# A hybrid decoder block on one core: first weights in quarters, taps read from E, operand fills in phases, and the branches' joins in the last pair's place

## The chip, the cores and the metric

The kernel runs on one core of one Trainium2 chip. The metric is the device time of one execution in microseconds (us): the median over several executions. Lower is better. One execution has also been recorded by the hardware profiler; its views are what this document quotes. The engines are PE (matrix multiplications), PEld (its weight loads, beside PE), DVE (elementwise work on two tensors), ACT (copies, scalings, activations), POOL (here it only issues DMAs and makes a few masks) and SP (here it only issues DMAs).

## The reference, cut to what matters

All tensors are float32, with 256 tokens of 4096 channels.

```python
h = rmsnorm(x, norm_w)
u_p, z_p, u_c, b_c, c_c, z_c, g_logit = split(h @ w_in)      # 20480 columns
y_pool = causal_multiscale_pool(u_p, pool_w, pool_scale) * silu(z_p)   # 2048
y_conv = b_c * conv3(c_c * u_c) * silu(z_c)                  # 2048, causal, width 3
br = [y_pool @ w_branch[0], y_conv @ w_branch[1]]            # 2 x 4096
gates = sigmoid(g_logit + gate_b)                            # 2 x 4096
merged = gates[0] * br[0] + gates[1] * br[1]
out = rmsnorm(x + merged @ w_out, final_norm_w)
```

## The kernel before

**Units and steps.** The work is cut into units of 1024 output columns, in this fixed order: cz0, cb0, cu0, cc0, the same four for cz1 (the convolution mixer's projections), pz0, pu0, pz1, pu1 (the pooling mixer's), g0_0, g1_0, ... g1_3 (eight units of gate logits), b0_0, b1_0, ... b1_3 (the two branch products, in turn for each quarter c of the columns), and o0 to o3 (the output product). A unit of w_in or w_out has 16 steps, a branch unit has 8. A step takes one weight tile of 256 rows by 1024 columns (1 MB, seen as four cells of 128x512) and multiplies it with the matching 256 channels of the 256 tokens.

**Float32 out of rounded halves.** Every float32 operand is split into a high part (rounded to the type that PE takes) and a low part (the rest). A product is three matmuls: high by high, high by low, low by high. ACT writes the high parts (`highs`, L185, through `act` at L54), DVE subtracts to get the low ones (`lows`, L189, through `tt` at L57). The parts lie in a ring of 15 cells. The weight tile itself lands in one of three raw slots of 1 MB.

**P and S steps.** A P step is 8 products, 24 matmuls. An S step is Strassen's form in the variant of Winograd: 7 products, 21 matmuls, but DVE must first make four sums of the weight cells (`parts`), of which ACT and DVE then make high and low parts too. A P operand takes 4 KB a partition in the arena, an S operand 7 or 8. The order of P and S within a unit is a string (`SIX4`, `EIGHT`, `B0`, `B1`, ...). The four E banks of PSUM (`sums`) take one output block each, the four F banks (`shared`) the products that serve several blocks. After the last S step ACT copies the F banks ("corners") into a raw slot, which the unit's `Join` object takes in the order of the loads; DVE makes three corner sums there, and adds them to the evacuated E banks (`combine`, L357).

**What sets the order.** All engines execute in the order in which the Python program issues instructions (`pin`). That order is made by hand: after each group of matmuls `after_group` (L919) evacuates banks that are complete, counts matmuls, and calls `tick` once for every 6. A tick pops one item of the queue of epilogue work and calls `pop_fill` (L702). Then `pump` (L875) issues what it may: the next weight load, when the raw slot's last user has been prepared, and the preparation (highs, sums, lows) of steps up to `limit`, which is four steps ahead, and only two at the last step of a unit that has `urgent` work (L932). `urgent` work is issued in `combine`, right behind the joins.

**The opening.** The first unit runs 16 P steps whose first operands are the scaled columns of x. For eight of them x is staged: ACT scales into `sa` (`x_scale`, L805), DVE makes four sums, a cast and a difference (`x_sums` and `fill_staged`, L811 and L655). `x_scale` of step j lies in the `pre` list of step j-1, ahead of its highs, and `x_sums` in its `mid` list, behind its lows (L825 to L830). The first weight tile is loaded in two halves (L866).

**Convolution taps.** At the end of cc0 and cc1 (`c_epi`, L462) PE transposes E into the F banks, two items apart; for each bank ACT writes the scaled middle tap to Y and four DVE instructions (`stt`, L69) add the other two taps, reading the bank in PSUM.

**Operand fills.** The operands of the branch and output products (8 + 8 + 16) go through DRAM and come back during the last gate unit and later. `Fill` objects fetch one into a stage (`sa`, later `sb` too) and, six or more ticks later, fill it whole: for an S operand four sums, a cast and a difference, all on DVE; for a P operand a cast on ACT and a difference on DVE. Only the head of the list is looked at. The last four operands of the output product are `Direct`: `fill_direct` (L664) makes them from Y in one go on DVE, without DRAM.

**Branches.** After b0_c DVE multiplies the branch with its gate into Y, and POOL stores that in DRAM (`p_d`, 1 MB). After b1_c DVE multiplies E with its gate, and POOL gathers `p_d` into E with an adding DMA. Then come transposes and the store to `m_d` (L596 to L619).

## Time and profile before

| what | value |
|---|---|
| median of 3 runs | 2462.22 us (2459.26 to 2463.23) |
| the profiled execution | 2464.99 us |
| its span, first to last instruction | 2463.3 us |
| mean granted clock of PE | 0.989 |
| matmul instructions of PE | 10515 |

The profile is of one execution. Its page has the busy time of each engine, a strip of 40 slices, and a chain of work followed back from the last instruction. The trace behind it answers by groups of instructions (busy time, mean length, the idle time before them and who ended it), by timeline (start, length, engine, line of the kernel, operation, output from input, count, and in brackets the idle time before the row and its releaser) and by windows (busy time and, in brackets, instructions of each engine in a stretch, then the granted clock of PE, the share of the DMA engines, and GB/s). Matmuls have L913, transposes L394, ACT's work L54, DVE's L57, L69 and L653.

### The profile page before, as it was taken

Reading aid. Unit: us, or ns where it says so; the run is one execution under the profiler, and the core shown is the slowest. Engines: PE = TensorE matmul, PEld = TensorE weight load, DVE = VectorE, ACT = ScalarE, POOL = GpSimd, SP = SyncE. Lnnn points to the kernel's source line nnn. Section 1 sums busy time; section 2 is a strip of 40 time slices with the busy share of each in tenths; the row PEclk is TensorE's granted clock in tenths of the full one; section 3 lists DMA queues with packets and bytes.
Section 4 is the critical chain, followed back from the end, with each engine's and each line's share of the span. In section 5 each row is a group of like instructions: output and inputs, shape, how many; then the busy total and the mean of one; then the engine's idle time right before and its main releaser. Section 6 shows DMA issues by size and latency. Waiting matters only on the chain.

```text
span 2463.3 us, 26875 instructions
## 1 busy us (share of the span) xinstructions
PE 2389.8 (97%) x10515; PEld 1966.2 (80%) x10515; DVE 2131.9 (87%) x1780; ACT 1410.6 (57%) x1358; POOL 91.8 (4%) x154
## 2 busy tenths in 40 slices
PE   7999999999999999999999999999999998999998
PEld 6888887888878888888888888887777776778886
DVE  6888889888988969969998899979868778899998
ACT  4656555656555656555666566655645545456664
POOL 0000000000000000000000000000000001000000
PEclk9999999999999999999999999999999999999999
DMA  7656457555645655655676567767667677658767
GB/s 280 250 205 222 179 183 254 201 193 208 225 182 204 232 189 193 224 196 189 247 256 229 197 241 258 239 205 260 233 239 282 205 251 244 215 179 267 243 220 269
DMA packets 83791, 553.36 MB, mean 225 GB/s; under 512 B 9552, under 2 KB 9552, under 8 KB 22096
## 3 DMA queue, kind: packets, MB, share of 16 engines
q1 hardware_dynamic: 68832, 484.47, 54.0%
q0 software_dynamic: 14400, 66.07, 9.5%
q8 instruction: 82, 1.34, 0.2%
q10 hardware_dynamic: 432, 1.11, 0.1%
q14 instruction: 45, 0.37, 0.0%
HBM read 522.25 MB, written 29.36 MB: 224 GB/s over the span
## 4 chain that ended last, share of the span: by engine, by line
PE 77%; DVE 12%; DMA 4%; ACT 4%; issue 3%; DVEq 0%; SPq 0%; ACTq 0%; POOL 0%; POOLq 0%
PE sums L913 57%; PE shared L913 18%; DVE ring L57 5%; DMA raw<-in_w_branch_dram 2%; ACT ring L54 2%; DVE parts L57 1%; DVE raw L57 1%; DVE E L57 1%; PE shared L570 1%; ACT raw L54 1%; ACT E L54 1%; DVE arena L57 1%; DMA raw<-in_w_in_dram 1%; DVE sa L57 0%; DVE Y L69 0%
## 5 line engine op out<-in xcount | busy, mean ns | idle before, releaser
L913 PE MATMUL sums<-ring,arena 128*128 128x512 f32 x7881 | 1850.7, 392 | 39.9 <-DVE ring L57 25.2
L913 PEld LDWEIGHTS sums<-ring,arena 128*128 128x128 f32 x7881 | 1486.7, 189 | 358.8 <-DVE ring L57 32.1
L57 DVE TENSOR_TENSOR ring<-raw,ring 128x2048 fp32r<-128x2048 f32 (+3 forms) x526 | 937.8, 1796 | 195.0 <-ACT ring L54 194.5
L54 ACT ACTIVATE ring<-raw 128x2048 fp32r<-128x2048 f32 (+3 forms) x526 | 790.8, 1520 | 521.9 <-PE sums L913 231.4
L54 ACT ACTIVATE ring<-parts 128x1024 fp32r<-128x1024 f32 (+1 forms) x402 | 399.7, 1009 | 360.2 <-DVE parts L57 323.0
L913 PE MATMUL shared<-ring,arena 128*128 128x512 f32 x2268 | 551.5, 392 | 18.5 <-DVE ring L57 9.8
L913 PEld LDWEIGHTS shared<-ring,arena 128*128 128x128 f32 x2268 | 426.5, 189 | 111.9 <-DVE ring L57 13.2
L57 DVE TENSOR_TENSOR ring<-parts,ring 128x2048 fp32r<-128x2048 f32 (+3 forms) x224 | 434.6, 1953 | 40.6 <-ACT ring L54 39.9
L57 DVE TENSOR_TENSOR parts<-parts,raw 128x512 f32<-128x512 f32 x378 | 262.0, 693 | 12.9
L57 DVE TENSOR_TENSOR parts<-raw 128x1024 f32<-128x1024 f32 x189 | 230.5, 1220 | 26.7 <-DMA raw<-in_w_branch_dram 21.3
L57 DVE TENSOR_TENSOR raw<-raw 128x512 f32<-128x512 f32 (+1 forms) x90 | 78.1, 868 | 14.7 <-ACT raw L54 12.7
L54 ACT ACTIVATE raw<-shared 128x512 f32<-128x512 f32 x120 | 64.2, 614 | 11.2 <-DVE ring L57 10.8
L54 ACT ACTIVATE E<-sums,rin 128x512 f32<-128x512 f32 x56 | 36.1, 689 | 25.4 <-PE sums L913 25.4
L69 DVE SCALAR_TENSOR_TENSOR E<-raw,rin,E 128x1024 f32<-128x1024 f32 x28 | 34.7, 1282 | 0.5
L54 ACT ACTIVATE E<-sums 128x512 f32<-128x512 f32 x44 | 24.6, 596 | 12.1 <-PE sums L913 11.2
L78 POOL DMA_DIRECT2D E<-in_rows_dram x16 | 13.8, 864 | 441.7 <-DVE E L69 439.5
L54 ACT ACTIVATE sa<-Y,par 128x256 f32<-128x256 f32 x16 | 7.3, 502 | 35.7 <-DVE extra L57 16.0
L57 DVE TENSOR_TENSOR arena<-sa,arena 128x512 fp32r<-128x512 f32 (+2 forms) x28 | 24.9, 890 | 2.5 <-ACT arena L54 1.8
L57 DVE TENSOR_TENSOR E<-E,raw 128x2048 f32<-128x2048 f32 x11 | 25.2, 2292 | 0.4
L57 DVE TENSOR_TENSOR E<-E,Y 128x2048 f32<-128x2048 f32 x11 | 25.2, 2290 | 0.3
L570 PE MATMUL shared<-ring 128*128 128x512 f32 x96 | 22.1, 389 | 0.0
L570 PEld LDWEIGHTS shared<-ring 128*128 128x128 f32 x96 | 18.0, 188 | 3.7
(114 smaller groups left out, 442.7 us busy)
## 6 DMA issues: line engine op xcount, KB each, us to landing
raw<-in_w_in_dram SPq DMA_DIRECT2D x319, 1024.0 KB, 4.8
raw<-in_w_branch_dram SPq DMA_DIRECT2D x64, 1024.0 KB, 6.2
raw<-in_w_out_dram SPq DMA_DIRECT2D x64, 1024.0 KB, 5.1
E<-in_rows_dram POOLq DMA_DIRECT2D x16, 512.0 KB, 10.0
gates_d<-E POOLq DMA_DIRECT2D x8, 1024.0 KB, 7.1
Y<-gates_d POOLq DMA_DIRECT2D x8, 1024.0 KB, 7.1
Y<-in_xc_dram SPq DMA_DIRECT2D x16, 256.0 KB, 5.2
E<-in_x_dram POOLq DMA_DIRECT2D x4, 1024.0 KB, 5.6
```

Source lines behind the costliest of these rows:

```text
L54: return pin(nc.scalar.activation(dst, src, func, **kw))
L57: return pin(nc.vector.tensor_tensor(out=dst, in0=a, in1=b, op=op))
L69: return pin(nc.vector.scalar_tensor_tensor(out=dst, in0=a, scalar=s, in1=b, op0=op0, op1=op1, **kw))
L78: return pin(nc.gpsimd.dma_start(dst, src, accum_op=ALU.add))
L570: pin(nc.tensor.matmul(o, a, b, start=(k, i) == (0, 0), stop=(k, i) == (3, 2)))
L913: pin(nc.tensor.matmul(ps, lhs, rhs, start=n == 0, stop=n == u.total[b] - 1))
```

## The change

1. The first weight tile is loaded in four quarters; its highs, lows and matmuls go cell by cell. `x_scale` moves from `pre` to `mid`, behind the lows of the step before. The squares of x's rows come two steps later, and the root goes to `mid` of the last step.
2. The taps: ACT first copies the four F banks to E, when the transposes of all of them are done; the taps read E.
3. Fills go in phases, one for each tick: an S operand has sums (DVE), a copy (ACT), a difference (DVE); a P operand the last two. `pop_fill` takes the first fill that may advance, not only the head. The direct fills are gone: all 16 operands of the output product go through `m_d`.
4. The arena loses its last region of 8 KB; a tile of its own, `last_pair`, stands for it. From b0_0 to b1_3 it holds the corners of b0_c (so that its join takes no raw slot), and then the gated b0_c, which DVE adds to E after b1_c. `p_d`, its stores and its adding gathers are gone. `urgent` no longer multiplies; the multiplications stand at the head of the epilogue. The lookahead at the last step of a branch unit is 3 and not 2.
5. `corner_sums` runs as soon as all corners are copied, not only in `combine`. A join that takes a raw slot stands one to two loads earlier among the loads where the unit before ends in P steps.
6. B1 is PSPSPSPP and not PSPPSPPS; the operands of branch two lie accordingly, three P operands in the places of two S operands (`("q", i)`).

The diff, cut to its core:

```diff
-B1 = "PSPPSPPS"
+B1 = "PSPSPSPP"
@@ Step.first, Step.rest (the same for lows)
                 if self is steps[0]:
-                    for i in (slice(0, 2), slice(2, 4)):
-                        highs(cells[i], self.q[:, i])
+                    for i in range(4):
+                        highs(cells[i:i + 1], self.q[:, i:i + 1])
@@ Step.groups
             if self is steps[0]:
                 for k in (1, 0):
-                    cells = self.cells[2 - 2 * k:4 - 2 * k]
-                    for i in range(3):
-                        for n in (1, 0):
+                    for n in (1, 0):
+                        cell = self.cells[2 * (1 - k) + 1 - n]
+                        h, l = high(cell), low(cell)
+                        for i in range(3):
                             for t in range(2):
@@
+    def corner_sums(u):
+        copy_corners(u)
+        if u.cornered or u.pending or u.join.slot is None or not u.closed(FB):
+            return
+        u.cornered = True
+        q = u.join.slot
+        add(q[:, 0], q[:, 2], q[:, 0])
+        add(q[:, 3], q[:, 0], q[:, 3])
+        sub(q[:, 0:2], q[:, 1:2].to_broadcast([P, 2, NH]), q[:, 0::3])
@@ conv_units, c_epi
-            items = gap(6)
+            def copy(j):
+                if j == 3:
+                    for i in range(4):
+                        act(chan(E)[:, 2 * i:2 * i + 2], bankview(i))
             def taps(j):
-                v, y = bankview(j), chan(Y)
+                v, y = chan(E)[:, 2 * j:2 * j + 2], chan(Y)
...
-            for f in transposes(E, taps):
-                items += [f, None]
+            items = gap(6) + pairs(transposes(E, copy)) + gap(2)
+            for j in range(4):
+                items += [lambda j=j: taps(j), None]
@@ branch_unit
             if n == 0:
-                return []
+                return gap(1) + [lambda: mul(parked_sum(), E, Y)]
...
-        def urgent():
-            if n == 0:
-                mul(Y, E, Y)
-                move(p_d[c], Y)
-            else:
-                mul(E, E, Y)
-                for t in range(2):
-                    gather(E[:, t], p_d[c][:, t])
+            def stored():
+                put(m_d[c], chan(Y))
+                merged[c] = now[0] + STORED
+            return [lambda: mul(E, E, Y), None, add_parked] + gap(11) + pairs(transposes(E, copy)) + [stored]
+        def add_parked():
+            add(E, E, parked_sum())
...
-        u.urgent = urgent
+        u.urgent, u.lead = (lambda: None), 3
+        if n == 0:
+            u.rotates = False
@@ class Fill (class Direct, fill_direct and fill_staged are gone)
+        def advance(self):
+            o, q = self.o, self.st[:, 0:self.o.n] if self.o.kind == "S" else self.st[:, 4:8]
+            if self.phase == 0 and o.kind == "S":
+                sums_s(self.st)
+                self.phase = 1
+            elif self.phase < 2:
+                act(o.view[:, 0], q)
+                self.phase = 2
+            else:
+                sub(o.view[:, 1], q, o.view[:, 0].bitcast(F32))
+                self.phase = 3
+                o.ready = True
+                fills.remove(self)
@@ pop_fill
+        for f in list(fills):
+            if f.at is not None and f.free() and (now[0] >= f.at + LANDING or f.o is force):
+                f.advance()
+                break
@@ opening
         if j in staged:
-            steps[j - 1].pre.append(item(x_scale, j))
-            steps[j - 1].mid.append(item(x_sums, j))
+            steps[j - 1].mid += [item(x_scale, j), item(x_sums, j)]
...
-        before(4 + 3 * c, square, c)
+        before(6 + 3 * c, square, c)
...
-    before(14, root)
+    steps[15].mid.append(item(root))
@@ loaded
-        loaded += mine[:3] + ([units[v - 1].join] if v and units[v - 1].s else []) + mine[3:]
+        before_it = units[v - 1] if v else None
+        at = 3
+        if before_it and before_it.main:
+            while before_it.main[len(before_it.main) - 1 - (3 - at)].kind == "P" and at > 1:
+                at -= 1
+        loaded += mine[:at] + ([before_it.join] if v and before_it.s and before_it.rotates else []) + mine[at:]
@@ issue_load
         if i == 0:
-            for k in range(2):
-                load(r[:, k * NU:(k + 1) * NU], s.src[:, k * NU:(k + 1) * NU])
+            for k in range(4):
+                load(r[:, k * NH:(k + 1) * NH], s.src[:, k * NH:(k + 1) * NH])
@@ after_group
-        copy_corners(u)
+        if u.s and u is not last:
+            corner_sums(u)
...
         if u.urgent and st is u.steps[-1]:
-            state["limit"] = state["now"] + 2
+            state["limit"] = state["now"] + u.lead
```

## The prediction

> **What bounds the kernel now.** I read the page's busy times first, then the chain of work, then the groups of instructions (for who ends PE's idle time), then windows over the whole span.

> ```profile
> PE 2389.8 (97%) x10515; PEld 1966.2 (80%) x10515; DVE 2131.9 (87%) x1780; ACT 1410.6 (57%) x1358; POOL 91.8 (4%) x154
> ```
> ```profile
> 118.05 7.48 PE sums L913 x33
> ```
> ```profile
> L913 PE MATMUL sums<-ring,arena 128*128 128x512 f32 x7881 | 1850.7, 392 | 39.9 <-DVE ring L57 25.2 <-ACT ring L54 9.8 <-ACT E L54 4.5
> ```
> ```profile
> L913 PE MATMUL shared<-ring,arena 128*128 128x512 f32 x2268 | 551.5, 392 | 18.5 <-DVE ring L57 9.8 <-DVE Y L69 8.7
> ```
> ```profile
> 40.00:360.00 320.00, 319.18 (x1413) 263.06 (x1412) 276.59 (x253) 188.87 (x184) 12.16 (x31) 1.00 0.60 220
> 360.00:400.00 40.00, 35.83 (x154) 28.47 (x153) 36.94 (x38) 17.73 (x20) 0.65 (x2) 0.91 0.53 196
> 400.00:700.00 300.00, 299.52 (x1329) 247.49 (x1328) 262.89 (x201) 177.88 (x164) 1.95 (x3) 1.00 0.58 208
> 700.00:740.00 40.00, 35.06 (x154) 28.09 (x153) 36.89 (x38) 17.77 (x21) 0.54 (x1) 0.96 0.54 197
> 740.00:1660.00 920.00, 919.82 (x4103) 761.88 (x4102) 809.85 (x633) 552.90 (x513) 30.14 (x41) 1.00 0.63 220
> 1660.00:1745.00 85.00, 77.17 (x328) 61.92 (x327) 76.45 (x74) 51.60 (x49) 8.70 (x15) 0.98 0.69 242
> 1745.00:2170.00 425.00, 394.73 (x1706) 321.72 (x1705) 341.24 (x294) 214.57 (x217) 26.23 (x41) 0.97 0.68 236
> ```

> PE is busy 97%. Its pace where nothing is missing is 7.48 / 33 = 0.2267 us a matmul (chain row). The number of matmuls does not change, so all that can be won is idle time, 39.9 + 18.5 = 58.4 us in the two groups, and the slower clock behind it. The windows say where that lies. I charge each instruction 0.2267 us and take the rest of the window as lost. From 40 to 360, 400 to 700 and 740 to 1660 nothing is lost. 360 to 400 and 700 to 740 lose 40 - 154 x 0.2267 = 5.1 each (end of cc0 and cc1, the taps). 1660 to 1745 (g1_3, start of b0_0) loses 85 - 74.4 = 10.6. 1745 to 2170 (all branches, start of o0) loses 425 - 386.7 = 38.3, of it 30.3 idle. The opening comes on top. Every edit is costed against these places.

> **The opening.** The weight loads' lengths are medians of the first 20 us; the timelines are of ACT, DVE and PE.

> ```profile
> 2.18 8.76 DMA Y<-in_xc_dram
> ```
> ```profile
> raw<-in_w_in_dram SPq DMA_DIRECT2D x3, 1024.0 KB, 10.6
> ```
> ```profile
> raw<-in_w_in_dram SPq DMA_DIRECT2D x2, 512.0 KB, 5.9
> ```
> ```profile
> 10.96 0.91 ACT L54 ACTIVATE sa<-Y,par 128x256 f32<-128x256 f32 x2 [6.15 <-DMA Y<-in_xc_dram]
> 11.77 1.99 ACT L54 ACTIVATE ring<-raw 128x1024 fp32r<-128x1024 f32 x2
> 18.48 0.91 ACT L54 ACTIVATE sa<-Y,par 128x256 f32<-128x256 f32 x2 [4.72 <-DVE extra L57]
> 19.30 3.70 ACT L54 ACTIVATE ring<-raw 128x2048 fp32r<-128x2048 f32 x2
> ```
> ```profile
> 15.12 1.02 DVE L57 TENSOR_TENSOR sa<-sa 128x128 f32<-128x128 f32 x4
> 16.18 0.63 DVE L653 CAST arena<-sa 128x896 fp32r<-128x896 f32 x1
> 16.84 1.09 DVE L57 TENSOR_TENSOR arena<-sa,arena 128x896 fp32r<-128x896 f32 x1
> ```
> ```profile
> 23.57 5.03 PE L913 MATMUL sums<-ring,arena 128*128 128x512 f32 x14 [1.82 <-DVE ring L57]
> ```

> Step 0's weights, issued ahead of the x columns of 2.18, are there by 2.2 + 5.9 = 8.1; their highs wait until 11.77 behind `x_scale`, which waited for those columns. The second `x_scale` (18.48) waits for DVE to empty `sa`, and step 1's highs (19.30) wait behind it. The new order puts step 0's highs ahead of `x_scale`, and step 1's ahead of the second one. Step 1 then has two inputs. Its x: 10.94, some 0.9 later for two more issues ahead of it, + 0.91 scale + 3.3 on DVE (the three rows and the extra column) = 16.1. Its weights: issued near 3.5, + 10.6 = 14.1, + 1.85 highs (half of 3.70) + 2.29 lows = 18.3. So step 1 is in full run at 18.3 and not at 23.57: 5.3, and with the 1.82 gap the clock dip behind it goes: **+6.5**, between +4 (quarters land no earlier than halves, x is later) and +8.5. The row fetch "later" changes nothing: POOL's first fetch has nothing to wait for in either order. SP's later loads wait for the same slots.

> **The taps.**

> ```profile
> 384.54 2.24 PE L913 MATMUL shared<-ring,arena 128*128 128x512 f32 x6 [1.99 <-DVE Y L69]
> 388.56 1.62 PE L913 MATMUL shared<-ring,arena 128*128 128x512 f32 x3 [1.78 <-DVE Y L69]
> ```
> ```profile
> 380.00:400.00 20.00, 16.23 (x61) 12.46 (x60) 19.72 (x23) 8.21 (x9) 0.09 (x1) 0.83 0.56 198
> ```
> ```profile
> L69 DVE SCALAR_TENSOR_TENSOR Y<-shared,par,Y 128x255 f32<-128x255 f32 (+1 forms) x32 | 14.5, 478 | 0.6
> ```
> ```profile
> E<-g_d POOLq DMA_DIRECT2D x2, 1024.0 KB, 7.6
> ```

> PE waits because the taps still read banks that it wants: 8.7 us in all four stalls (the "DVE Y L69" of the second group). The copies free the banks, so these stalls go. But the 16 taps of a unit are still 7.6 us of DVE, and DVE has only 0.28 us free in these 20: what is late next is the lows behind the taps. E is also in use longer: POOL's load of `g_d` into E waited for the transposes and now waits for the last tap on DVE. It takes 7.6, and the multiplication that needs it stands 6 ticks behind, 36 matmuls or 8.2 us, and lows behind that on DVE; up to 2 us of new wait there. I take half of what the two places lose: **+5.5**, between +1 (the whole wait moves to the ring) and +12 (20 - 61 x 0.2267 = 6.2 lost in this window, twice). [...]

> **Fills in phases, g1_3 and the start of b0_0.**

> ```profile
> 1733.75 6.55 PE L913 MATMUL sums<-ring,arena 128*128 128x512 f32 x21 [4.52 <-ACT E L54]
> ```
> ```profile
> 1730.67 0.65 ACT L54 ACTIVATE arena<-sa 128x512 fp32r<-128x512 f32 x1
> 1731.19 1.93 ACT L54 ACTIVATE ring<-raw 128x2048 fp32r<-128x2048 f32 x1
> 1732.99 2.44 ACT L54 ACTIVATE E<-sums,rin 128x512 f32<-128x512 f32 x4
> ```

> An S fill loses its 0.63 cast on DVE and gets a copy on ACT instead, 0.65 x 896/512 = 1.1. What matters is the order: DVE sums, ACT copy, DVE difference, with ACT in program order. Here PE waits 4.52 because the E banks are evacuated behind a P fill's copy and one highs of 1.93. In the new order an S fill's copy stands in that place, and its sums stand on DVE behind two lows (4.5) and the corner sums (2.67, below): queued behind this one ACT instruction are highs of step 2 and the evacuation that PE waits for. I expect 8 to 10 where 4.52 stands, and small stalls in g1_3 (85 - 77.17 - 4.52 = 3.3 now) to change places: **-6.5**, between -10 and +1 (the copy finds its sums done).

> **Branch boundaries.**

> ```profile
> 1780.43 2.67 DVE L57 TENSOR_TENSOR raw<-raw 128x512 f32<-128x512 f32 x3
> 1783.14 2.29 DVE L57 TENSOR_TENSOR E<-E,raw 128x2048 f32<-128x2048 f32 x1
> 1785.47 2.29 DVE L57 TENSOR_TENSOR Y<-E,Y 128x2048 f32<-128x2048 f32 x1
> 1787.68 4.49 DVE L57 TENSOR_TENSOR ring<-raw,ring 128x2048 fp32r<-128x2048 f32 x2
> ```
> ```profile
> 1790.02 11.17 PE L913 MATMUL sums<-ring,arena 128*128 128x512 f32 x48 [1.89 <-DVE ring L57]
> ```
> ```profile
> 2069.89 14.67 PE L913 MATMUL sums<-ring,arena 128*128 128x512 f32 x53 [6.99 <-DVE ring L57]
> ```
> ```profile
> 2159.25 3.78 PE L913 MATMUL shared<-ring,arena 128*128 128x512 f32 x8 [6.02 <-DVE ring L57]
> ```

> PE waits 1.89 for step 2's lows, which stand behind 2.67 + 2.29 + 2.29 of join and gate. With the lead of 3 they stand ahead of the last two, 4.58: this stall goes. Next late is step 3, whose load comes after the join has given its slot back; where b0 ends its join has none now, and the load comes without delay; where b1 ends it still does. `p_d` gone takes 8 MB of transfers from these bursts and costs DVE four adds of 2.29, covered by its 425 - 341.24 = 84 idle in the stretch, except in its last unit. Of the 38.3 lost from 1745 on, 6.99 and 6.02 are idle in b1_3 and o0; of the other 17.3 idle and 8 of slow clock some 14 lie at the boundaries up to b0_3: **+11**, between +4 and +15.

> **b1_3 and o0.** b1_3's 6.99 stands behind fills on DVE and a late load; the fills are as many as before, plus the add. o0's start also gets the pattern of b0_0: **-2.5** (-6 to +5). In o0 6.02 comes from four direct fills ahead of the lows; they go through DRAM now, and are done ticks later and before the steps that use them. With the clock behind it and the neighbouring stalls: **+9.5** (5 to 11).

> **At nothing:** corner sums ahead of lows at the boundaries of the other units, and earlier joins there; PE has 0.18 idle in the 920 us from 740 on, and DVE 110 to cover 2.67 each time; without that cover each boundary would cost up to 2.67. B1's order has the same 5 P and 3 S.

> **Sum:** 6.5 + 5.5 - 6.5 + 11 - 2.5 + 9.5 = 23.5. The profiled execution took 2464.99 us (span 2463.3), 2.8 over the median; 2464.99 - 23.5 = 2441.5, and against the median 2462.22 - 23.5 = **2438.7**.

> **The rivals.**
> - *The starts don't stall.* If DVE has run ahead, the S fills' copies find their sums done, and the two starts cost nothing extra; the rest then comes near its upper ends: 6.5 + 8 + 13 + 10.5 + 0 = 38, **2424**. For it: ACT is 57% busy. Against: DVE has 8.6 free of 85 in that stage.
> - *It does not do what it says.* DVE stays the bound: taps +1, boundaries +4, fills -6.5, o0 +5, and only the opening 6.5 is real: 10, **2452**. For it: 25.2 of the 39.9 already end at DVE's ring.
> - *Slower: the phases stop DVE.* Each of 13 S fills (5 for branches, 8 for the output product) makes DVE wait for ACT's copy behind one highs: 1.1 + 1.93 - 0.63 = 2.4, where DVE has no reserve; with the slow clock as in the taps' window (6.2 lost on 3.77 idle, 1.6 times) 3.8 of PE. All other gains make 32.5 without the two start terms; from 9 of 13 fills on it is slower. All 13: 50 lost, 17 net, **2479**. Against: DVE has 84 free in the branches.

> **How the numbers follow.** Forecast 0.45 (2431 to 2447 by itself), starts don't stall 0.22, DVE stays the bound 0.18, phases 0.15. The range 2418 to 2460 leaves out the last rival and the far ends. About 0.2%, 4.9 us, is what a measurement of this kernel tells from no change. Faster: the first two and two thirds of the third, 0.79; same: the rest of it and a few fills, 0.08; slower: 0.13.

> **What would show it.** Right: step 1 in full run near 18; no wait on "DVE Y" at L69; b0_0's first matmul later behind "ACT E" by 4 to 5 than now; 1.89 at b1_0's step 2 gone; no stall of 6 in o0. Wrong: a gap at the taps' place with releaser "DVE ring" as large as before, DVE idle behind "ACT arena" in many rows, or new idle time from 740 to 1660.

## The result, and the profile after

| | before | after |
|---|---|---|
| median of 4 runs | 2461.56 us (2459.26 to 2463.23) | 2442.16 us (2441.45 to 2444.01) |
| profiled execution, span | 2464.99, 2463.3 | 2441.96, 2440.2 |

The ratio of after to before is 0.9923, 95% interval 0.9906 to 0.994: 19.4 us faster by the medians. The two profiled executions differ by 23.0, since that of before is 3.4 above its median and that of after is not.

The page's busy times of after, and the two groups of PE that carried the idle time (the page's costliest groups):

```profile
PE 2382.4 (98%) x10515; PEld 1959.1 (80%) x10515; DVE 2130.3 (87%) x1756; ACT 1430.8 (59%) x1380; POOL 86.3 (4%) x148
...
L935 PE MATMUL sums<-ring,arena 128*128 128x512 f32 x7515 | 1760.0, 391 | 38.2 <-ACT E L54 17.9
...
L935 PE MATMUL shared<-ring,arena 128*128 128x512 f32 x2100 | 509.5, 391 | 5.0 <-DVE ring L57 5.0
```

From the view of waits (us in all, times, the longest):

```profile
PE sums L935 <- ACT E L54: 17.9, 3, 8.7
PE sums L935 <- DVE ring L57: 15.8, 12, 3.6
```

PE's idle time in the two groups fell from 58.4 to 43.2, and its make-up changed: "DVE Y" is gone, "DVE ring" fell from 25.2 + 9.8 to 15.8 + 5.0, and "ACT E", the evacuation of the E banks, went from 4.5 to 17.9. To see where the time came from, I took from both traces the moment at which PE begins the same step, and subtracted. Steps are counted from 0, and the last column is the prediction's term.

| PE begins | before | after | gained so far | in this part | forecast |
|---|---|---|---|---|---|
| cb0 (the opening is over) | 108.36 | 102.00 | 6.4 | +6.4 | +6.5 |
| cz1 | 356.10 | 349.91 | 6.2 | -0.2 | 0 |
| cz1, step 7 (taps of cc0 are over) | 401.93 | 392.05 | 9.9 | +3.7 | +2.75 |
| pz0 | 696.55 | 686.92 | 9.6 | -0.3 | 0 |
| pz0, step 7 (taps of cc1 are over) | 742.37 | 729.15 | 13.2 | +3.6 | +2.75 |
| g1_3 | 1641.39 | 1629.35 | 12.0 | -1.2 | 0 |
| b1_0 (g1_3 and b0_0 are over) | 1777.54 | 1772.94 | 4.6 | -7.4 | -6.5 |
| b1_3 | 2052.32 | 2036.62 | 15.7 | +11.1 | +11 |
| o0 | 2107.24 | 2093.51 | 13.7 | -2.0 | -2.5 |
| o1 | 2206.05 | 2182.51 | 23.5 | +9.8 | +9.5 |
| end of the span | 2463.28 | 2440.23 | 23.05 | -0.5 | 0 |

The places that were put at nothing lose 2 in all, and no stall over 0.3 stands there. The matmuls that read an operand in `last_pair` are slower in the changed kernel:

```profile
L935 PE MATMUL sums<-ring,last_pair 128*128 128x512 f32 x366 | 89.8, 396 | 0.0
```

From 740 to 1660 one begins every 0.234 us, the others every 0.227, as all did before. Over the 534 of them (366 and 168) that is 3.8 us, an estimate from these two figures: a price of part 4 that the prediction did not have.

The opening, in the timelines of ACT and of PE after:

```profile
14.24 1.91 ACT L54 ACTIVATE ring<-raw 128x2048 fp32r<-128x2048 f32 x1 [1.60 <-DMA raw<-in_w_in_dram]
```
```profile
18.53 4.82 PE L935 MATMUL sums<-ring,arena 128*128 128x512 f32 x14 [1.82 <-DVE ring L57]
```

Step 1 is in full run at 18.53, 23.57 before. Its highs now wait for the weights alone, which land just ahead of 14.24. The taps, in PE's timeline and in windows:

```profile
385.39 1.43 PE L935 MATMUL sums<-ring,arena 128*128 128x512 f32 x5 [0.86 <-DVE ring L57]
386.66 1.07 PE L935 MATMUL shared<-ring,arena 128*128 128x512 f32 x4
389.42 2.11 PE L935 MATMUL shared<-ring,arena 128*128 128x512 f32 x8 [1.69 <-DVE ring L57]
```
```profile
380.00:400.00 20.00, 17.44 (x76) 13.78 (x76) 19.76 (x20) 10.79 (x10) 0.56 (x1) 1.00 0.63 240
```

The stalls of 1.99 and 1.78 behind "DVE Y" became 0.86 and 1.69 behind "DVE ring", two steps later. DVE is as full as before (19.76 of 20), and the granted clock is 1.00 where it was 0.83. At the starts of b0_0 and o0 the stall grew; this is PE and then ACT and DVE at b0_0:

```profile
1726.79 13.58 PE L935 MATMUL sums<-ring,arena 128*128 128x512 f32 x49 [8.67 <-ACT E L54]
```
```profile
1717.38 1.08 ACT L54 ACTIVATE raw<-shared 128x512 f32<-128x512 f32 x2
1723.41 0.95 ACT L54 ACTIVATE arena<-sa 128x896 fp32r<-128x896 f32 x1 [4.96 <-issue]
1724.27 1.89 ACT L54 ACTIVATE ring<-raw 128x2048 fp32r<-128x2048 f32 x1
1726.07 1.25 ACT L54 ACTIVATE E<-sums,rin 128x512 f32<-128x512 f32 x2
```
```profile
1717.52 2.29 DVE L57 TENSOR_TENSOR ring<-raw,ring 128x2048 fp32r<-128x2048 f32 x1 [0.48 <-ACT ring L54]
1719.73 2.67 DVE L57 TENSOR_TENSOR raw<-raw 128x512 f32<-128x512 f32 x3
1722.32 1.01 DVE L57 TENSOR_TENSOR sa<-sa 128x128 f32<-128x128 f32 x4
1726.19 2.29 DVE L57 TENSOR_TENSOR ring<-raw,ring 128x2048 fp32r<-128x2048 f32 x1 [2.86 <-ACT ring L54]
```

The fill's copy (arena from sa) starts the moment DVE has its sums done (1722.32 + 1.01), and DVE came to them behind a lows and the corner sums. "Issue" is the page's word for a wait that it has no releaser for; DVE's row shows what it was. Behind the copy stand a highs and then E. DVE in turn idles 2.86 for that highs. At o0 a copy (0.95, behind DVE) and a highs (1.89) stand ahead of E in the same way; ahead of both, ACT waits 7.99 for a load of `w_out`, and DVE for the highs of that load:

```profile
2093.51 11.79 PE L935 MATMUL sums<-ring,arena 128*128 128x512 f32 x44 [7.91 <-ACT E L54]
```

### The profile page after: what moved, and what is told of

The parts are those of the page before. It is cut to its first block, busy times and chain, and to the rows that moved or that the text cites. A ratio compares the mean times of both kernels' runs of the same rounds, so it can differ in the third digit from the quotient of the medians.

```text
span 2440.2 us, 26870 instructions
## 1 busy us (share of the span) xinstructions
PE 2382.4 (98%) x10515; PEld 1959.1 (80%) x10515; DVE 2130.3 (87%) x1756; ACT 1430.8 (59%) x1380; POOL 86.3 (4%) x148
## 5 line engine op out<-in xcount | busy, mean ns | idle before, releaser
L935 PE MATMUL sums<-ring,arena 128*128 128x512 f32 x7515 | 1760.0, 391 | 38.2 <-ACT E L54 17.9
L935 PEld LDWEIGHTS sums<-ring,arena 128*128 128x128 f32 x7515 | 1411.4, 188 | 340.7 <-DVE ring L57 21.9
L57 DVE TENSOR_TENSOR ring<-raw,ring 128x2048 fp32r<-128x2048 f32 (+3 forms) x526 | 938.8, 1796 | 186.4 <-ACT ring L54 182.7
L54 ACT ACTIVATE ring<-raw 128x2048 fp32r<-128x2048 f32 (+3 forms) x526 | 790.7, 1519 | 491.5 <-PE sums L935 259.5
L54 ACT ACTIVATE ring<-parts 128x1024 fp32r<-128x1024 f32 (+1 forms) x403 | 399.9, 1007 | 355.4 <-DVE parts L57 322.8
L935 PE MATMUL shared<-ring,arena 128*128 128x512 f32 x2100 | 509.5, 391 | 5.0 <-DVE ring L57 5.0
L57 DVE TENSOR_TENSOR ring<-parts,ring 128x2048 fp32r<-128x2048 f32 (+3 forms) x225 | 434.9, 1945 | 50.3 <-ACT ring L54 49.4
L935 PEld LDWEIGHTS shared<-ring,arena 128*128 128x128 f32 x2100 | 395.4, 189 | 91.0 <-DVE ring L57 8.7
L57 DVE TENSOR_TENSOR parts<-parts,raw 128x512 f32<-128x512 f32 x378 | 262.0, 693 | 12.9
L57 DVE TENSOR_TENSOR parts<-raw 128x1024 f32<-128x1024 f32 x189 | 230.6, 1220 | 8.0 <-DMA raw<-in_w_in_dram 7.1
L935 PE MATMUL sums<-ring,last_pair 128*128 128x512 f32 x366 | 89.8, 396 | 0.0
L935 PEld LDWEIGHTS sums<-ring,last_pair 128*128 128x128 f32 x366 | 68.9, 188 | 16.5
L57 DVE TENSOR_TENSOR raw<-raw 128x512 f32<-128x512 f32 (+1 forms) x78 | 67.7, 868 | 11.1 <-ACT raw L54 9.3
L54 ACT ACTIVATE raw<-shared 128x512 f32<-128x512 f32 x104 | 55.8, 606 | 2.8 <-DVE ring L57 2.1
L54 ACT ACTIVATE E<-sums,rin 128x512 f32<-128x512 f32 x56 | 36.4, 686 | 25.5 <-PE sums L935 25.4
L935 PE MATMUL shared<-ring,last_pair 128*128 128x512 f32 x168 | 41.6, 396 | 0.0
L935 PEld LDWEIGHTS shared<-ring,last_pair 128*128 128x128 f32 x168 | 31.6, 188 | 7.7
L69 DVE SCALAR_TENSOR_TENSOR E<-raw,rin,E 128x1024 f32<-128x1024 f32 x28 | 34.7, 1280 | 0.2
L54 ACT ACTIVATE arena<-sa 128x512 fp32r<-128x512 f32 (+2 forms) x16 | 12.2, 760 | 32.9 <-DMA sa<-y_d 15.1
L54 ACT ACTIVATE arena<-sb 128x512 fp32r<-128x512 f32 (+1 forms) x15 | 11.3, 754 | 25.8 <-DVE sb L57 20.9
L57 DVE TENSOR_TENSOR E<-E,Y 128x2048 f32<-128x2048 f32 x11 | 25.2, 2290 | 0.3
## 6 DMA issues: line engine op xcount, KB each, us to landing
raw<-in_w_in_dram SPq DMA_DIRECT2D x319, 1024.0 KB, 4.8
raw<-in_w_branch_dram SPq DMA_DIRECT2D x64, 1024.0 KB, 4.9
raw<-in_w_out_dram SPq DMA_DIRECT2D x64, 1024.0 KB, 5.0
E<-in_rows_dram POOLq DMA_DIRECT2D x16, 512.0 KB, 11.3
gates_d<-E POOLq DMA_DIRECT2D x8, 1024.0 KB, 8.3
Y<-gates_d POOLq DMA_DIRECT2D x8, 1024.0 KB, 6.2
E<-in_x_dram POOLq DMA_DIRECT2D x4, 1024.0 KB, 6.5
```

Source lines behind the costliest of these rows:

```text
L54: return pin(nc.scalar.activation(dst, src, func, **kw))
L57: return pin(nc.vector.tensor_tensor(out=dst, in0=a, in1=b, op=op))
L69: return pin(nc.vector.scalar_tensor_tensor(out=dst, in0=a, scalar=s, in1=b, op0=op0, op1=op1, **kw))
L935: pin(nc.tensor.matmul(ps, lhs, rhs, start=n == 0, stop=n == u.total[b] - 1))
```

## The experiments

All times are medians, beside runs of the kernel before on the same chip; the changed kernel's own ratio is 0.9923.

| run | edit | us | ratio to before (95%) | before |
|---|---|---|---|---|
| e1_opening_only | before + opening, row fetches left | 2455.21 | 0.9976 (0.9966 to 0.9985) | 2461.22 |
| e5_opening | before + opening | 2455.31 | 0.9977 (0.9967 to 0.9986) | 2460.76 |
| e2_taps_psum | after, taps from PSUM | 2447.12 | 0.9945 (0.993 to 0.996) | 2461.22 |
| e3_copy_dve | after, S fills' copy on DVE | 2431.73 | 0.9883 (0.9868 to 0.9898) | 2461.22 |
| e4_hold | after, no fill in a unit's last step | 2437.98 | 0.9907 (0.9891 to 0.9924) | 2461.22 |
| e8_evac_first | after, lookahead 2 at two unit ends | 2436.19 | 0.9896 (0.9881 to 0.9911) | 2460.76 |
| e6_raw_slot | after, b0's join in a raw slot | 2441.81 | 0.992 (0.9905 to 0.9935) | 2460.76 |
| e7_through_dram | after, gated b0 through DRAM | 2449.7 | 0.9949 (0.9934 to 0.9963) | 2460.76 |
| e9_lead2 | after, lookahead 2 in all branches | 2439.11 | 0.9912 (0.9894 to 0.993) | 2459.97 |
| e10_mul_later | after, b0's multiplication 7 ticks later | 2441.24 | 0.9921 (0.9905 to 0.9937) | 2459.97 |
| e11_late_corners | after, corner sums in combine | 2450.11 | 0.9962 (0.9949 to 0.9976) | 2459.97 |
| e12_combined | after, four edits | 2424.98 | 0.9857 (0.9839 to 0.9874) | 2459.97 |

### The opening alone (e1, e5)

The edit is part 1 of the change put into the kernel before. The first run left the row fetches where they were, so its squares are of the wrong rows; the second moves them with the squares.

```diff
-        before(2 + 3 * c, fetch_rows, c)
+        before(4 + 3 * c, fetch_rows, c)
```

> The kernel before with the opening's part of the change alone (quarter loads, cells one by one, scaling behind the lows, squares and root later). My theory: the opening is worth about 7.5 us by itself (the changed kernel reaches step 1's full run at 18.53 and not 23.57, and the small waits up to 76 us go), so about 2454, and the rest of the kernel is as before, with the same gaps at the taps, at b0_0 (4.52) and in b1_3 (6.99). Rival: the first unit is limited by the weight loads, and what is won at 18 us is lost again by 80 us; then within 2 us of before, 2461.

> The kernel before with the opening's part of the change alone, now with the row fetches moved two steps as well, as the changed kernel has them (the first run of this part left the fetches where they were, so that its squares read rows of the wrong block). My theory: the opening is worth 6 to 8 us by itself: about 2454.5. Rival: moving the fetches too takes nothing and gives nothing, and the earlier run's 6 was spread between runs: above 2458.

Both give 5.5 to 6.0 us, and in the traces of e5 and of before PE begins cb0 6.2 earlier. After that the opening's gain is kept to the end. Moving the fetches is worth nothing that shows. The rest of e5's profile has the larger stalls of before at the same steps.

### The taps from PSUM again (e2)

The line below is the core of it. With it the four copies of ACT go, and the transposes stand two items apart again, each followed by its taps, as before.

```diff
-                v, y = chan(E)[:, 2 * j:2 * j + 2], chan(Y)
+                v, y = bankview(j), chan(Y)
```

> The changed kernel with its taps reading the PSUM banks as before. My theory: the banks' release is what PE waited for, so the four stalls with releaser DVE Y come back (8.7 us in place of 5.6 at the ring) and the clock dip with them: 5 to 7 us slower than the changed kernel, about 2448.5. Rival: the 16 taps' time on DVE is the cause and PE waits as long at the ring: within 1.5 us of the changed kernel, 2442 to 2443.5.

5.0 us slower than the changed kernel, with no overlap between the runs (2446.39 to 2447.96 against 2441.45 to 2444.01), and the four stalls behind "DVE Y" are back. So the release of the banks was it, and not only the taps' time on DVE. But the dip of the clock is no part of these 5.0 in the trace. This window of e2 holds stalls of 2.03 and 2.39 and has a granted clock of 1.00 (more in the last section):

```profile
370.00:390.00 20.00, 15.59 (x70) 12.28 (x68) 19.65 (x27) 12.34 (x16) 0.57 (x1) 1.00 0.55 209
```

### The S fills' copy on DVE, and the fills held back (e3, e4)

```diff
-                act(o.view[:, 0], q)
+                (copy if o.kind == "S" else act)(o.view[:, 0], q)
```

> The changed kernel with the S fills' rounding copy on DVE again, still one phase for each tick. My theory: the 8.67 before b0_0 and the 7.91 before o0 are evacuations of E that stand on ACT behind a fill's copy, which waits for DVE's sums. Without the copy on ACT both fall to 4 to 5, and DVE pays 0.63 for each of 13 fills where it has time: 5 to 8 us faster than the changed kernel, about 2435.5. Rival: the evacuation waits for highs whose weights come late; then both gaps stay above 7 and the time is within 1.5 us, or up to 3 slower by the 8 us that DVE gets.

10.4 us faster than the changed kernel, more than I expected. Where PE begins the same steps, 3.4 of it are won by b0_0 and 9.3 by o0. PE at b0_0 in e3, and ACT ahead of it:

```profile
1723.43 6.88 PE L935 MATMUL sums<-ring,arena 128*128 128x512 f32 x22 [6.09 <-ACT E L54]
```
```profile
1720.89 1.91 ACT L54 ACTIVATE ring<-raw 128x2048 fp32r<-128x2048 f32 x1 [6.76 <-DMA raw<-in_w_branch_dram]
1722.71 1.25 ACT L54 ACTIVATE E<-sums,rin 128x512 f32<-128x512 f32 x2
```

The copy is gone from ACT, and yet 6.09 stays: ACT sat 6.76 on a highs whose weights had not landed, with the evacuation behind it. My rival was half right; there are two blockers in the one queue.

```diff
         for f in list(fills):
+            if held[0] and force is None:
+                break
...
+            held[0] = st is u.steps[-1]
             run_step(u, st)
```

> The changed kernel with no fill advanced during the last step of a unit (until its join is issued); the copies stay on ACT. My theory: the copy in front of the evacuation is the cause, so both starts fall to about 4.5 (one highs of 1.9 stays ahead of the evacuation) and the fills, some four ticks later, are still in time: 6 to 9 us faster, about 2434.5. Rival: the fills have no time to spare; what is won at the starts comes back as waits of DVE or of PE for an operand within the next two steps, in b0_0 or b1_3: within 2 us of the changed kernel.

4.2 faster. The wait before b0_0 falls to 5.38, but the one before o0 grows from 7.91 to 9.51: there ACT's queue is held by a highs that waits 4.89 for its load, and E's evacuation stands behind it:

```profile
2085.72 1.91 ACT L54 ACTIVATE ring<-raw 128x2048 fp32r<-128x2048 f32 x1 [4.89 <-DMA raw<-in_w_out_dram]
2087.54 2.04 ACT L54 ACTIVATE E<-sums 128x512 f32<-128x512 f32 x4
```

So the theory held at one start and not at the other.

### The evacuation ahead of the third step's highs (e8)

```diff
-        u.urgent, u.lead = (lambda: None), 3
+        u.urgent, u.lead = (lambda: None), 2 if (n, c) == (1, 3) else 3
...
+        if (n, c) == (1, 3):
+            units[-1].urgent = lambda: None
```

> The changed kernel with a lookahead of 2 in the last step of g1_3 and of b1_3 alone, so that the highs of the next unit's third step stand behind the evacuation of E and not ahead; the fills' copies stay on ACT. With the copy on DVE the two starts still took 6.09 and 5.01, and highs whose weights had just landed stood ahead of the evacuation. My theory: those highs are the rest of the wait: 8.67 at b0_0 and 7.91 at o0 fall by 2 to 5 each, 5 us faster than the changed kernel, about 2437. Rival: the copy alone is the limit here, the highs go in its shadow: 1.9 less at each start and the lows of the third step later by as much, within 2 us of the changed kernel.

6.0 faster. In PE's timeline of e8 the two starts:

```profile
1726.72 8.48 PE L937 MATMUL sums<-ring,arena 128*128 128x512 f32 x26 [5.82 <-ACT E L54]
```
```profile
2089.28 10.98 PE L937 MATMUL sums<-ring,arena 128*128 128x512 f32 x40 [3.56 <-ACT E L54]
```

From 8.67 and 7.91 to 5.82 and 3.56. At b0_0 what is left is the fill's copy, which still waits for DVE.

### What made the branch boundaries faster (e6, e7, e9, e10, e11)

The first two take back one half of part 4 each.

```diff
         u.urgent, u.lead = (lambda: None), 3
-        if n == 0:
-            u.rotates = False
```

> The changed kernel with the join of b0_c in a raw slot again, taken in the order of the loads; the gated branch stays in the last pair's place, and nothing goes through DRAM. My theory: the slot is what made b1's early steps late, so the loads of b1_c's steps 2 and 3 wait for the join, and 1.5 to 3 us come back at each of the four b1 starts: 2442 + 8 = 2450. Rival: the order (lead of 3, multiplication behind the lows) took the stall away and the slot does nothing: within 1.5 us of the changed kernel.

Nothing: 2441.81, and PE begins b1_3 within 0.7 us of the changed kernel. The join's slot, from which I had expected the later loads to come in time, is worth nothing here.

```diff
-                return gap(1) + [lambda: mul(parked_sum(), E, Y)]
+                return gap(1) + [lambda: (mul(parked_sum(), E, Y), move(p_d[c], parked_sum()))]
...
-            add(E, E, parked_sum())
+            for t in range(2):
+                gather(E[:, t], p_d[c][:, t])
```

> The changed kernel with the gated b0_c stored in DRAM and gathered into E by an adding DMA again, as before, instead of the add on DVE; the join stays in the last pair's place. My theory: the transfers are hidden in the first steps of the next unit, and DVE saves 2.29 four times, of which only b1_3's counts: within 2 us of the changed kernel, 2440.5 to 2444. Rival: the 8 MB meet the weight loads (their median to landing fell from 6.2 to 4.9 us with the change), and highs that wait for a load come back: 4 us or more slower, with ACT ring waiting on the branch weights as before (123.9 us, 49.0 with the change).

7.5 slower by the medians, but PE does not lose it in either of the ways I named. The profiled execution, the fastest of the four, shows 5.0 of it. In PE's timeline of e7, and in the view of waits:

```profile
1840.40 0.98 PE L423 MATMUL shared<-ident,E 128*128 128x128 f32 x7 [2.04 <-DMA E<-p_d]
```
```profile
ACT ring L54 <- DMA raw<-in_w_branch_dram: 61.4, 19, 7.5
...
PE shared L423 <- DMA E<-p_d: 6.4, 4, 2.0
```

PE's transposes wait 6.4 in all for the gather. ACT waits 61.4 for branch weights, 49.0 in the changed kernel and 123.9 before, so the transfers alone do not bring those waits back. They do slow the loads beside them. Here are three loads at b0_2 in the kernel before, beside the two gathers (1921 to 1934), and then three issued close together in the changed kernel (1909 to 1912):

```profile
raw<-in_w_branch_dram SPq DMA_DIRECT2D x3, 1024.0 KB, 12.0
```
```profile
raw<-in_w_branch_dram SPq DMA_DIRECT2D x3, 1024.0 KB, 6.9
```

In e7 the branch weights' median to landing is 5.9, and 4.9 in the changed kernel, but PE's waits for "ACT ring" in `sums` are 4.9 in all, and 4.4 in the changed kernel. Part of the transposes' wait is this run's own, since the transposes stand earlier after b1 than in the kernel before (the gap there was 15 items from the gather on, here it is 11).

```diff
-        u.urgent, u.lead = (lambda: None), 3
+        u.urgent, u.lead = (lambda: None), 2
```

> The changed kernel with the lookahead of 2 again in the last step of every branch unit. The slot of the join made no difference and the way through DRAM acted by late transposes, so the gain of 8 at the branch boundaries should be the order on DVE. My theory: with 2 the lows of the next unit's step 2 stand behind E's add again (2.29; the multiplication is later by itself now), so the waits on DVE's ring at the b1 starts and at b0's step 4 partly come back: 3 to 6 us slower, about 2446.5. Rival: the order inside the epilogue (multiplication behind the lows) was enough, and with 2 the evacuations before b1_0 and o0 come earlier (1.30 and some of 7.91 saved): 1 to 4 us faster than the changed kernel.

3.1 faster than the changed kernel by the medians (the kernel before was 1.6 faster in that set too, and the intervals overlap). PE's stall at b1_0 goes back to step 2 and shrinks:

```profile
1785.41 8.50 PE L935 MATMUL sums<-ring,arena 128*128 128x512 f32 x29 [1.77 <-DVE ring L57]
```

So the lead of 3 earned nothing that shows; at b1_0 it only moved the wait from step 2 to step 3. This is the changed kernel's row, and DVE ahead of it:

```profile
1792.20 1.88 PE L935 MATMUL sums<-ring,arena 128*128 128x512 f32 x5 [2.78 <-DVE ring L57]
```
```profile
1778.49 2.67 DVE L57 TENSOR_TENSOR last_pair<-last_pair 128x512 f32<-128x512 f32 x3
1781.08 2.28 DVE L57 TENSOR_TENSOR ring<-raw,ring 128x2048 fp32r<-128x2048 f32 x1
1783.28 2.29 DVE L57 TENSOR_TENSOR E<-E,last_pair 128x2048 f32<-128x2048 f32 x1
1785.60 2.29 DVE L57 TENSOR_TENSOR last_pair<-E,Y 128x2048 f32<-128x2048 f32 x1
1787.81 1.22 DVE L57 TENSOR_TENSOR parts<-raw 128x1024 f32<-128x1024 f32 x1
```

DVE is busy without a break from the corner sums on, and the sums of step 3 (parts) stand behind the multiplication.

```diff
-                return gap(1) + [lambda: mul(parked_sum(), E, Y)]
+                return gap(8) + [lambda: mul(parked_sum(), E, Y)]
```

> The changed kernel with the gate's multiplication after b0_c seven ticks later (8 empty items ahead of it, not 1). My theory: this 2.29 on DVE ahead of step 3's sums is what is left of the wait at step 3 of each b1 (2.78, 0.58, 0.58, 3.61 us with releaser DVE ring): most of the 7.5 go, 4 to 7 us faster, about 2436.5. Rival: the stall at step 3 comes from its weights or from the join's add; moving the multiplication moves the wait one step on: within 1.5 us.

The stall at b1_0's step 3 falls as expected:

```profile
1791.39 1.43 PE L935 MATMUL sums<-ring,arena 128*128 128x512 f32 x5 [0.47 <-DVE ring L57]
```

But the time stays, 2441.24. New waits for "ACT E" stand before b0_1 (1.59), b0_2 (0.77) and b0_3 (0.79), and the one before o0 is 8.70. The DVE work of a branch pair is not less, and the wait moved to where it is late next.

```diff
-        if u.s and u is not last:
-            corner_sums(u)
+        copy_corners(u)
```

> The changed kernel with the corner sums only in the combining again, in every unit. My theory: they cost and bring nothing in the units of w_in and w_out, where PE has no idle time, and in the branches they only change places with lows of the same length: within 1.5 us of the changed kernel. Rival: they took an idle time of DVE at every boundary (DVE waits for corners behind its lows), so without them small waits come back from 740 to 1660 and in the branches: 3 us or more slower.

8.0 slower, and my theory is wrong. DVE in e11 at the same place:

```profile
1778.71 2.29 DVE L57 TENSOR_TENSOR ring<-parts,ring 128x2048 fp32r<-128x2048 f32 x1 [1.52 <-ACT ring L54]
1781.98 2.29 DVE L57 TENSOR_TENSOR ring<-raw,ring 128x2048 fp32r<-128x2048 f32 x1 [0.97 <-ACT ring L54]
1784.19 2.67 DVE L57 TENSOR_TENSOR last_pair<-last_pair 128x512 f32<-128x512 f32 x3
```
```profile
1795.83 1.69 PE L935 MATMUL sums<-ring,arena 128*128 128x512 f32 x5 [3.99 <-DVE ring L57]
```

The two do not only change places. Behind the sums' lows DVE has nothing to do for 0.97 us, since the next highs are not there; the corner sums, whose corners are, fill that hole when they come first. Without it the stall at step 3 is 3.99 and not 2.78, 1.77 and not 0.58 at b1_1 and b1_2, 6.36 and not 3.61 at b1_3. From the start of g0_0 to that of g1_3, where PE has no stall, e11 falls back 1.0 us against before, and the changed kernel 0.9: there the sums' place costs nothing. At b0_0 it does: with the corner sums out of the way, the fill's sums and so its copy come sooner, and E's wait is 5.52 and not 8.67. The profiled execution of e11, the slowest of its five, is 11.6 behind that of the changed kernel: 2.1 in the opening, which the edit leaves as it is, 3.6 between b1_0 and b1_3, and most of the rest in b1_3 and o0.

### All together (e12)

```diff
-                if self is steps[0]:
+                if self in steps[:2]:
```

and the edits of e3, e8 and e10.

> The changed kernel with four edits: the S fills' copy on DVE, a lookahead of 2 in the last step of g1_3 and b1_3, the multiplication after b0_c seven ticks later, and step 1's highs and lows in four pieces as well as step 0's. My theory: the copy alone gave 10.4 and the lookahead alone 6; together the starts go from 8.67 and 7.91 to some 3 each, which is 4 to 5 less than with the copy alone; the multiplication gives 4 to 6 more and the opening's pieces 1.5 to 3: 2431.7 - 10.5, about 2421. Rival: the gains overlap, since DVE is what all of them wait for in the end (the stalls move to its ring): 2428 to 2432.

2424.98: 17.2 under the changed kernel, 35 under before. PE in e12 at b0_0 (no wait in brackets) and at o0:

```profile
1714.91 5.40 PE L937 MATMUL sums<-ring,arena 128*128 128x512 f32 x23
```
```profile
2077.05 13.22 PE L937 MATMUL sums<-ring,arena 128*128 128x512 f32 x57 [2.77 <-ACT E L54]
```

Either blocker alone leaves 5.8 to 6.1 at b0_0; with both gone nothing is left. Step 1 is in full run at 16.71. The time is 4 above my 2421, between my theory and my rival: behind b0_0's start stands a new stall of 2.77 on DVE's ring at its step 5, and the waits for "ACT E" that e10 brought before b0_1, b0_2 and b0_3 are here too (1.83, 0.86 and 0.60).

## Why the prediction was right

The forecast was 23.5 us, 2438.7 in 2418 to 2460; measured were 19.4 us and 2442.16. The terms were read from the profile of before, and by the two profiles, which differ by 23.0, they come out closer than by the medians. Step by step:

- **The opening**, +6.5: 6.4 in the profiles, 5.5 by e5. The chain that I wrote (weights at 14.1, full run at 18.3) is what the trace shows: 14.24 and 18.53, 5.0 earlier than before. The other 1.2 of the term was wrong: the gap of 1.82 and the dip behind it are still there (a granted clock of 0.50 from 18.0 to 21.4, and in the kernel before from 23.5 to 26.9). That the term fits is luck there: 1.1 comes behind step 7, where a stall of 0.82 of before is gone.
- **The taps**, +5.5: 7.3 in the profiles, 5.0 by e2. The release of the banks counts, and what is late next is the ring, as foreseen (5.6 us of new stalls for 8.7). Wrong was to charge the clock dip to the stall. It stands in the profile of before (0.83 and 0.91), in one of e5's two places (1.00 and 0.91), and in none of e2's (1.00 and 1.00), with stalls as long. At cz1 e5, with the taps of before but no dip, is 1.5 us faster than before over this part. So 1.99 went with a dip in the trace of before, and 2.03 and 2.39 went without one in e2 (last section); the dips may be part of why the profiles differ by 3.6 us more than the medians.
- **Fills in phases at the two starts**, -6.5 and -2.5: -7.4 and -2.0, with 8.67 where I wrote 8 to 10. e3 shows the cause: with the copy on DVE 10.4 come back. I missed that the highs whose weights come late are a second blocker (e3, e8). And the -2.0 is a hit by luck: it is +6.8 up to step 7 of b1_3, where stalls of 6.99 and 1.85 became 1.29 and 3.61, and -8.7 from there to o0.
- **Branch boundaries**, +11: 11.1, but two of my reasons fell. The slot is worth nothing (e6), the lead of 3 nothing or a little less (e9). The DRAM traffic did delay the loads beside it, as I had supposed, but in e7 this does not reach PE; its round trip cost PE's transposes there. What I did not price in the branches, corner sums as soon as the corners are there, carries 8 us of the whole by the medians (e11), in the profiles 3.6 of these 11.1. I priced them at nothing in the other units, where that is right, but for the start of b0_0. So 11.1 for 11 is in part luck.
- **o0**, +9.5: 9.8. The 6.02 behind four direct fills is gone; no stall over 0.85 is left inside o0. No run takes the direct fills back alone, so this cause is read from the two traces and not shown by an experiment.

*Still open:* the stalls at step 4 of b0_1, b0_2 and b0_3 (0.69, 1.82 and 1.83 us in the profile of before) are gone in every variant of the changed kernel. What PE waited for is in the trace of before: step 4's highs waited 13.3 to 13.8 us on ACT for their weights. At b0_2:

```profile
1933.67 1.91 ACT L54 ACTIVATE ring<-raw 128x2048 fp32r<-128x2048 f32 x1 [13.80 <-DMA raw<-in_w_branch_dram]
```

This load was issued 10.9 us after the unit's start, when the lows that stood on DVE behind the join and the gate's multiplication were done, and took 9.9 us beside the gathers. In the changed kernel it is issued 4.7 us after the start. e7 has the gathers and a landing of 12.3, issues the load as early, and has no stall there. So the earlier issue is enough to end these stalls. Which part brings it is not shown: B1's order, which ends in two P steps so that its corners are ready two steps early, the earlier join in the order of the loads, or the multiplication out of combine. None of these was tried alone; I had priced the order at nothing.

## What to carry to other kernels

Look at what stands ahead of a PSUM evacuation in its engine's queue, at the end of each stage: here an instruction that waited there for DVE (a copy of 0.95 us) or for a load (a highs of 1.91) stopped PE, and the two hid much of each other's cost until both were gone (b0_0 here: 8.67 with both, 6.09 and 5.82 with one, no wait with neither). Where an engine has holes in a full stretch, order by when inputs are ready; that was worth 8 us here with the same work. A stall that was moved off one step came back at another (e9, e10), since the engine behind it had as much to do, so price the stretch and not the step.

## What the runs showed of the hardware that I had not expected

These are two neighbouring cells of before, around its stalls of 1.99 and 1.78, and two stretches as long of e2, around its 2.03 and 2.39 (PE's busy time stands first behind the length, the granted clock third from the end):

```profile
381.91:385.32 3.41, 1.42 (x6) 0.86 (x5) 3.30 (x7) 0.78 (x1) 0.00 (x0) 1.00 0.37 156
385.32:388.73 3.41, 1.63 (x5) 0.84 (x4) 3.34 (x6) 0.00 (x0) 0.00 (x0) 0.50 0.34 46
```
```profile
375.80:379.21 3.41, 1.73 (x8) 1.11 (x6) 3.27 (x8) 1.91 (x3) 0.00 (x0) 1.00 0.69 288
379.21:382.63 3.42, 1.63 (x6) 1.05 (x6) 3.38 (x5) 0.00 (x0) 0.00 (x0) 1.00 0.01 2
```

The 1.99 of before lies whole in the first cell, and the second is at half clock. The two stretches of e2 hold 1.68 and 1.79 of idle time, so neither of its longer stalls lies whole in one of them, and the clock is 1.00 in both. In the changed kernel the clock is at half from 1721.28 on, within the 8.67 before b0_0, for three cells in a row, which gives 0.74 over these 20 us:

```profile
1720.00:1740.00 20.00, 13.21 (x49) 10.77 (x50) 12.61 (x17) 8.55 (x9) 2.80 (x4) 0.74 0.60 182
```
